# A state-space mixer in steps of two positions, inside a two-block transformer kernel

## The chip, the cores and the metric

The kernel runs on one core of one Trainium2 chip, in one launch. The metric is the device time in microseconds; the median of three runs is given. Engines are named as in the profile: PE is TensorE (matmuls; PEld its weight loads), DVE is VectorE, ACT is ScalarE, POOL is GpSimd, SP is SyncE, whose queue issues the weight loads from HBM.

## The reference, cut to what matters

Two transformer blocks run over one sequence of 256 positions of width 2048, in float32. The second block has three branches: a gated MLP over positions, the state-space mixer (S5) and a stick-breaking attention. In the mixer, 64 groups of 16 channels each drive 64 complex diagonal states:

```python
dt = jnp.exp(log_dt)[:, None]
mag = jnp.exp(lam_re * dt)
ab_re = mag * jnp.cos(lam_im * dt)          # the step a, complex
ab_im = mag * jnp.sin(lam_im * dt)
...
bu_re = jnp.einsum('blgh,gph->blgp', u, bb_re)
bu_im = jnp.einsum('blgh,gph->blgp', u, bb_im)
# associative scan over positions: s[t] = a * s[t-1] + bu[t]
_, _, s_re, s_im = lax.associative_scan(combine, (a_re, a_im, bu_re, bu_im), axis=1)
y = (jnp.einsum('blgp,ghp->blgh', s_re, c_re) - jnp.einsum('blgp,ghp->blgh', s_im, c_im))
y = y.reshape(bsz, seq, S5_WIDTH) + d * xin
g = jax.nn.gelu(y)
out = g * jax.nn.sigmoid(g @ w_glu + b_glu)
```

## The kernel before, in words

Every wide product is made from float32 weights split in two parts: ACT writes the high half `wh` in a reduced matmul format (fp32r; L213), DVE the rest, `wl` (L214), and PE adds three products, weights' high by activations' high and low, and low by high. Weights come in pieces of 512 KB that SP's queue loads.

In the first part of the second block (`block2`) the projection's columns are worked off in the order `ORDER2`: U and W for the gated MLP, C for the mixer's input, V and Q for the attention, G for gates. Each of these steps yields after a few matmuls with the PE time that they were planned at. Between the steps the loop in `block2` hands out other work by that planned time: one step of the mixer (`states`, the generator `rest`) for every 3.9 us (`RS`), and one step of the attention or gating chains for every 0.52 us (`RC`). What then stands where on each engine's queue is set by a planner that puts the instructions in order by a simulated timeline. Each engine works its queue in order.

The mixer (`s5`) keeps two groups side by side on the 128 partitions, so there are 32 blocks of 128 states (real and imaginary part each), in 8 groups of four (`ct`). A setup computes steps, powers of the rotation (`ek`) and input matrices `bb`. Then, for each group `ct`, `prepare` spreads the matrices B and C into block form by ACT and PE transposes, splits them in high and low, and POOL builds the table `tab` of the rotation's powers for 128 positions by doubling. For each block `i`:

- `drive(i)`: PE multiplies the block's input (`xin`, 32 channels as high and low halves on 64 partitions, 256 positions) by B: 4 matmuls of 256 columns into a PSUM bank `bu`.
- `scan(i)`: DVE turns the drive back by the table (two products over 128x512, an add and a subtract over 128x256). What is left is a real recurrence with factor |a|, which DVE's scan instruction runs (L2002). The table reaches over 128 positions, so the 256 are scanned in two halves, with three small instructions that carry the state over (L1998 to L2000): four scans. POOL turns the result forward again with two products over 128x512 (L2004, L2005).
- `result(i)`: an add and a subtract over 128x256 finish the turn; for two blocks of four (`CO` = 2) DVE does them, for the others POOL. ACT writes the high half `sh`, POOL the low half `sl` (L2017). PE multiplies both by C into the group's bank: 4 matmuls of 256 columns. After the fourth block DVE adds the bank to `y` (L2029, four instructions).

PSUM banks for all of this come from `pmx`, four that go round, shared with the attention and gating chains.

Of the kernel before, what the change touches and what calls it, by code (L numbers as in the profile page):

```python
# [18 lines left out]
T = 256  # L19
# [9 lines left out]
def _consts():  # L29
    p = np.arange(128)[:, None]  # L30
    f = np.arange(128)[None, :]
    t = np.arange(T)[None, :]
    c = {}
    c["ident"] = p == f
    c["bd64"] = (p // 64) == (f // 64)
    for d in (128, 64):
        half = d // 2
        inv = np.float32(10000.0) ** (-np.arange(half, dtype=np.float32) * np.float32(2.0 / d))
        ang = np.arange(T, dtype=np.float32)[:, None] * inv.astype(np.float32)[None, :]
        cos = np.cos(ang).astype(np.float32).T  # L40
# [18 lines left out]
    c["tril"] = p >= f  # L59
    c["ntril"] = np.where(p >= f, -1.0e30, 0.0)  # L60
# [10 lines left out]
C3 = ("geq", "strict", "tril", "ntril", "half", "odd")  # L71
# [44 lines left out]
class Ker:  # L116
# [1366 lines left out]
    LO, CO = (0, 2)  # L1483
# [157 lines left out]
    def gmlp(self, y, w_in, vp, chains):  # L1641
# [62 lines left out]
    def sb(self, y, w_in, vp, chains):  # L1704
# [29 lines left out]
        def heads(j, q, k, pre):  # L1734
# [15 lines left out]
            for i, w in enumerate(work):  # L1750
# [6 lines left out]
                nc.vector.tensor_add(dg(zs), dg(zs), b2(c["ntril"]))  # L1757
# [41 lines left out]
    def s5(self, y, w_in, st):  # L1799
# [6 lines left out]
        with ExitStack() as s1:  # L1806
# [91 lines left out]
        def cols(j):  # L1898
# [17 lines left out]
        mats = []  # L1916
        for i in range(2):

            mats.append([p.tile([128, 640], F32R, name=f"C{i}{a}") for a in range(2)])
            for m in mats[i]:  # L1920
                G.memset(m.bitcast(F32), 0.0)

        def prepare(ct):

            tabs[ct] = tab = p.tile([128, 2, 4, H], F32, name="tab", bufs=2)
            Cm = mats[ct % 2]
            B = [[p.tile([128, 2, 128], F32R, name=f"B{x}{a}", bufs=2) for x in "hl"] for a in range(2)]
            blocks[ct] = B, Cm
            for a in range(2):
                rb = p.tile([128, 4, 2, 2, 16], F32, name="rb")  # L1930
                rc = p.tile([128, 2, 64], F32, name="rc")
                for e in range(2):
                    nc.scalar.activation(rb[:, :, :, e], bb[:, a, 4 * ct:4 * ct + 4][:, :, None, :].to_broadcast([128, 4, 2, 16]),
                                         AF.Copy, scale=c["half"][:, e:e + 1])
                    nc.scalar.activation(rc[:, e], cc[:, a, ct], AF.Copy, scale=c["odd"][:, e:e + 1])
                ps = self.pmx()
                for g in range(2):
                    nc.tensor.transpose(ps[:, ts(g, 128)], rb[:, 2 * g:2 * g + 2].rearrange("p k d e h -> p (k d e h)"),
                                        self.ident)
                nc.tensor.transpose(ps[:, 256:384], rc.rearrange("p e n -> p (e n)"), self.ident)  # L1940
                self.split(*(t.rearrange("p g n -> p (g n)") for t in B[a]), ps[:, 0:256])
                ch = Cm[a].rearrange("p (k n) -> p k n", k=4)[:, :, 0:32]
                pc = ps[:, 256:384].rearrange("p (k n) -> p k n", k=4)
                nc.scalar.activation(ch, pc, AF.Copy)
                for g, o in ((0, 64), (1, 256)):
                    k2 = slice(2 * g, 2 * g + 2)
                    V.tensor_sub(Cm[a][:, o:o + 320].rearrange("p (k n) -> p k n", k=2)[:, :, 0:32], pc[:, k2],
                                 ch[:, k2].bitcast(F32))
# [3 lines left out]
            for k in range(7):  # L1952
                n = 1 << k
                er, ei = (ek[:, k, a, 4 * ct:4 * ct + 4][:, :, None].to_broadcast([128, 4, n]) for a in range(2))
# [11 lines left out]
        hv = lambda t: t.rearrange("p a (c t) -> p a c t", c=2)  # L1966
        w2 = lambda nm, bufs: p.tile([128, 2, T], F32, name=nm, bufs=bufs)
        bus, posts, ypss = {}, {}, {}

        def drive(i):  # L1970

            ct, k = divmod(i, 4)
            B, rows, g = blocks[ct][0], slice(64 * (k % 2), 64 * (k % 2) + 64), k // 2
            xi = xins[ct // 2][rows, g, ts(ct % 2, T)]
            bu = bus[i] = self.pmx()
            for a in range(2):
                for x in range(2):
                    self.mm(bu[:, ts(a, T)], B[a][x][rows, g], xi, start=a == x == 0, stop=a == x == 1)

        def tables(i):  # L1980
            ct, k = divmod(i, 4)
            tab = tabs[ct]
            return [tab[:, a, k][:, None, None, :].to_broadcast([128, 2, 2, H]) for a in range(2)]

        def scan(i):
            cb, sb = tables(i)
            bv = bus.pop(i).rearrange("p (a t) -> p a t", a=2)
# [18 lines left out]
            posts[i] = b1, z  # L2006

        def result(i):
# [5 lines left out]
            sh = p.tile([128, 2, T], F32R, name="sh", bufs=self.SB)  # L2014
            sl = p.tile([128, 2, T], F32R, name="sl", bufs=self.SB)
# [4 lines left out]
            yps, Cm = ypss[ct], blocks[ct][1]  # L2020
            for a in range(2):
                for x in (sh, sl):
                    self.mm(yps[:, ts(k // 2, T)], Cm[a][:, ts(k, 128)], x[:, a], start=k % 2 == 0 and a == 0 and x is sh,
                            stop=k % 2 == 1 and a == 1 and x is sl)
            if k == 3:
                for g in range(2):
# [145 lines left out]
```

## Time and profile before

| | before |
|---|---|
| median of 3 runs | 2947.54 us (2946.69 to 2952.38) |
| the profiled execution's own time | 2951.56 us |
| its span, first to last instruction | 2949.4 us |
| PE busy | 2832.4 us (96%) |
| DVE busy | 2105.3 us (71%) |
| ACT busy | 1612.5 us (55%) |
| POOL busy | 455.1 us (15%) |
| mean granted PE clock | 0.990 |

An engine's busy time is the time covered by its instructions. Matmuls are pipelined and their ends are modelled, so a busy PE is not PE at its peak. The shares are means over stages that differ; the mixer's stage lies from about 1330 us to 1762 us of the span.

### The profile page before, as it was taken

Reading aid. Unit: us, or ns where it says so; the run is one execution under the profiler, and the core shown is the slowest. Engines: PE = TensorE matmul, PEld = TensorE weight load, DVE = VectorE, ACT = ScalarE, POOL = GpSimd, SP = SyncE. Lnnn points to the kernel's source line nnn. Section 1 sums busy time; section 2 is a strip of 40 time slices with the busy share of each in tenths; the row PEclk is TensorE's granted clock in tenths of the full one; section 3 lists DMA queues with packets and bytes.
Section 4 is the critical chain, followed back from the end, with each engine's and each line's share of the span. In section 5 each row is a group of like instructions: output and inputs, shape, how many; then the busy total and the mean of one; then the engine's idle time right before and its main releaser. Section 6 shows DMA issues by size and latency. Waiting matters only on the chain. (4 is left out here: it accounts for less than half of the span.)

```text
span 2949.4 us, 45262 instructions
## 1 busy us (share of the span) xinstructions
PE 2832.4 (96%) x17284; PEld 2493.9 (85%) x17284; DVE 2105.3 (71%) x2898; ACT 1612.5 (55%) x2161; POOL 455.1 (15%) x623
## 2 busy tenths in 40 slices
PE   8999999997999999998888789999999999999998
PEld 8998989876887788787677789999988888888887
DVE  7685876647998999898999986555555654456554
ACT  6466466536777777765444445444445553345443
POOL 1111111011000000018898840000000000000000
PEclk9999999998999999999999999999999999999999
DMA  6444443484989999864434336666556666666665
GB/s 196 132 118 120 119 118 104 128 285 150 380 296 350 378 379 357 305 176 142 122 115 122 100 110 196 187 187 186 186 186 197 189 188 194 194 189 186 192 193 171
DMA packets 400512, 576.77 MB, mean 196 GB/s; under 512 B 25032, under 2 KB 252624, under 8 KB 400160
## 3 DMA queue, kind: packets, MB, share of 16 engines
q1 hardware_dynamic: 397632, 567.74, 59.6%
q0 software_dynamic: 2624, 6.06, 0.8%
q8 instruction: 137, 2.24, 0.3%
q14 instruction: 87, 0.71, 0.1%
q10 hardware_dynamic: 32, 0.01, 0.0%
HBM read 571.64 MB, written 2.10 MB: 195 GB/s over the span
## 5 line engine op out<-in xcount | busy, mean ns | idle before, releaser
L214 DVE TENSOR_TENSOR wl<-raw,wh 128x1024 fp32r<-128x1024 f32 (+1 forms) x917 | 1133.7, 1241 | 624.5 <-ACT wh L213 604.6
L213 ACT ACTIVATE wh<-raw 128x1024 fp32r<-128x1024 f32 (+1 forms) x917 | 965.2, 1055 | 900.8 <-PE acc L223 686.6
L223 PE MATMUL acc<-hx,wh 128*128 128x256 f32 (+3 forms) x5280 | 1149.8, 306 | 0.5 <-ACT hx L347 0.2
L223 PE MATMUL acc<-hx,wl 128*128 128x256 f32 x3152 | 890.1, 284 | 13.1 <-DVE wl L214 13.0
L223 PEld LDWEIGHTS acc<-hx,wh 128*128 128x128 f32 (+2 forms) x5280 | 849.7, 189 | 55.4 <-issue 8.0
L223 PEld LDWEIGHTS acc<-hx,wl 128*128 128x128 f32 x3152 | 592.8, 188 | 24.1 <-DVE wl L214 15.3
L214 DVE TENSOR_TENSOR wl<-rx,wh 128x1024 fp32r<-128x1024 f32 x159 | 191.3, 1223 | 26.9 <-ACT wh L213 13.6
L223 PE MATMUL acc<-wl,xgh 128*128 128x512 f32 x512 | 201.2, 394 | 2.5 <-DVE wl L214 2.5
L223 PE MATMUL acc<-wh,xgh 128*128 128x512 f32 x512 | 200.1, 391 | 2.9 <-ACT wh L213 2.9
L223 PE MATMUL acc<-wh,xgl 128*128 128x512 f32 x512 | 200.4, 392 | 0.0
L223 PE MATMUL acc<-wh,al 128*128 128x512 f32 x512 | 199.2, 389 | 0.0
L223 PE MATMUL acc<-wh,ah 128*128 128x512 f32 x512 | 199.2, 389 | 0.0
L213 ACT ACTIVATE wh<-rx 128x1024 fp32r<-128x1024 f32 x159 | 167.6, 1061 | 55.9 <-PE acc L223 36.4
L223 PE MATMUL acc<-wl,ah 128*128 128x512 f32 x512 | 179.2, 389 | 0.0
L223 PE MATMUL mx<-wh,act 128*128 128x512 f32 x512 | 140.3, 394 | 1.5 <-DVE act L220 0.8
L223 PE MATMUL acc<-wh,hx 128*128 128x512 f32 x384 | 122.6, 402 | 0.0
L223 PEld LDWEIGHTS acc<-wl,xgh 128*128 128x128 f32 x512 | 96.2, 188 | 25.4 <-DVE wl L214 5.3
L223 PEld LDWEIGHTS mx<-wh,act 128*128 128x128 f32 x512 | 96.6, 189 | 23.2 <-DVE act L220 1.2
L223 PEld LDWEIGHTS acc<-wh,xgh 128*128 128x128 f32 x512 | 96.2, 188 | 23.1 <-ACT wh L213 4.1
L223 PEld LDWEIGHTS acc<-wl,ah 128*128 128x128 f32 x512 | 96.1, 188 | 20.0
L223 PEld LDWEIGHTS acc<-wh,xgl 128*128 128x128 f32 x512 | 96.2, 188 | 19.9
L223 PEld LDWEIGHTS acc<-wh,ah 128*128 128x128 f32 x512 | 96.1, 188 | 19.9
(589 smaller groups left out, 4149.2 us busy)
## 6 DMA issues: line engine op xcount, KB each, us to landing
raw<-in_w_in_dram SPq DMA_DIRECT2D x304, 512.0 KB, 3.7
raw<-in_w_mlp_in_dram SPq DMA_DIRECT2D x128, 512.0 KB, 3.8
raw<-in_w_mlp_out_dram SPq DMA_DIRECT2D x128, 512.0 KB, 3.8
raw<-in_w_e_gate_dram SPq DMA_DIRECT2D x80, 512.0 KB, 6.0
raw<-in_w_e_down_dram SPq DMA_DIRECT2D x77, 512.0 KB, 6.0
raw<-in_w_e_up_dram SPq DMA_DIRECT2D x75, 512.0 KB, 5.7
raw<-in_w_out_dram SPq DMA_DIRECT2D x57, 512.0 KB, 3.8
rx<-in_w_e_up_dram SPq DMA_DIRECT2D x53, 512.0 KB, 6.4
```

What stands on the lines that cost most here:

```text
L213: self.lasth = nc.scalar.activation(h[:, :n], raw[:, :n], AF.Copy).ins
L214: self.lastl = nc.vector.tensor_sub(l[:, :n], raw[:, :n], h[:, :n].bitcast(F32)).ins
L223: return self.nc.tensor.matmul(out, lhsT, rhs, start=start, stop=stop)
```

## The change

The mixer steps over pairs of positions. States are kept at even positions only (0, 2, ..., 254): 128 of them, so one table covers them all and the second half with its joins goes away. The recurrence becomes s[2t] = a² s[2t-2] + (a B) u[2t-1] + B u[2t], so the drive takes the even inputs and the odd ones before them, with matrices B and a B, on all 128 partitions. The output at even positions is C s[2t], at odd ones (C a) s[2t] + (C B) u[2t+1], from matrices C a one step later and a direct product D = C B of the odd input. `xin` gets a new layout: odd inputs, shifted by one pair, on partitions 0 to 63, even ones on 64 to 127. `prepare` makes more matrices and asks for five PSUM banks where it asked for two. The result's add and subtract are done by DVE for all blocks (`CO` = 4). Two constants of the attention are dropped, one of them replaced by a scalar times the mask `geq` at L1757, the scratch for descriptors of POOL's DMAs is made smaller, and the loads of `br` and `bi` are cut in two.

```diff
-    LO, CO = (0, 2)
+    LO, CO = (0, 4)
...
-                nc.vector.tensor_add(dg(zs), dg(zs), b2(c["ntril"]))
+                nc.vector.scalar_tensor_tensor(dg(zs), b2(c["geq"]), -1.0e30, dg(zs), op0=OP.mult, op1=OP.add)
...
+            ab = p.tile([128, 2, 32], F32, name="ab")
+            V.tensor_mul(ab, ek[:, 0], sc[:, 0:1].to_broadcast([128, 2, 32]))
+            m2 = p.tile([128, 32], F32, name="m2")
+            V.tensor_mul(m2, sc[:, 0], sc[:, 0])
...
-            nc.gpsimd.dma_start(br, A["s5_b_re_2"][0].rearrange(pat, a=2))
-            nc.gpsimd.dma_start(bi, A["s5_b_im_2"][0].rearrange(pat, a=2))
+            for s in (0, 16):
+                for t_, n in ((br, "re"), (bi, "im")):
+                    nc.gpsimd.dma_start(t_[:, s:s + 16], A[f"s5_b_{n}_2"][0, 2 * s:2 * s + 32].rearrange(pat, a=2))
...
+            ka = lambda k: ab[:, k][:, :, None].to_broadcast([128, 32, 16])
+            V.tensor_mul(bb[:, 0, 0], b0, ka(0))
+            V.tensor_mul(t3, b1, ka(1))
+            V.tensor_sub(bb[:, 0, 0], bb[:, 0, 0], t3)
+            V.tensor_mul(bb[:, 1, 0], b1, ka(0))
+            V.tensor_mul(t3, b0, ka(1))
+            V.tensor_add(bb[:, 1, 0], bb[:, 1, 0], t3)
...
+            xins[j] = xin = p.tile([128, 2, 4, H + 2], F32R, name="xin", bufs=self.XB)
+            G.memset(xin[0:64, :, :, 0:1].bitcast(F32), 0.0)
             for k in range(4):
-                o = 64 * (k % 2)
-                h, l, f = slice(o, o + 32), slice(o + 32, o + 64), slice(32 * k, 32 * k + 32)
-                nc.scalar.activation(xin[h, k // 2], xn[f], AF.Copy)
-                V.tensor_sub(xin[l, k // 2], xn[f], xin[h, k // 2].bitcast(F32))
+                xn = yj[32 * k:32 * k + 32].rearrange("p a (c t) -> p a c t", t=2)
+                for o, c0, t in ((0, 1, 1), (64, 0, 0)):
+                    h, l = (xin[o + d:o + d + 32, :, k, c0:c0 + H] for d in (0, 32))
+                    nc.scalar.activation(h, xn[:, :, :, t], AF.Copy)
+                    V.tensor_sub(l, xn[:, :, :, t], h.bitcast(F32))
...
+                for k in range(4):
+                    nc.tensor.transpose(ps[:, ts(k, 128)], rb[:, k].rearrange("p t d e h -> p (t d e h)"), self.ident)
+                self.split(*(t.rearrange("p g n -> p (g n)") for t in B[a]), ps)
+                ps = self.pmx()
+                nc.tensor.transpose(ps[:, 0:128], rc.rearrange("p e n -> p (e n)"), self.ident)
+                nc.scalar.activation(cf[:, a, :, 0], ps[:, 0:128].rearrange("p (k n) -> p k n", k=4), AF.Copy)
+            yield
+
+            ar, ai = (ab[:, x, 4 * ct:4 * ct + 4][:, :, None].to_broadcast([128, 4, 32]) for x in range(2))
+            tc_ = p.tile([128, 4, 32], F32, name="tc")
+            for o, x, y0, op in ((0, ar, ai, G.tensor_add), (1, ai, ar, G.tensor_sub)):
+                G.tensor_mul(tc_, cf[:, 0, :, 0], x)
+                G.tensor_mul(cf[:, o, :, 1], cf[:, 1, :, 0], y0)
+                op(cf[:, o, :, 1], cf[:, o, :, 1], tc_)
+            self.split(*(t.rearrange("p a k t n -> p (a k t n)") for t in C), cf.rearrange("p a k t n -> p (a k t n)"))
+            ps = self.pmx()
+            for k in range(4):
+                for a in range(2):
+                    self.mm(ps[0:64, ts(k, 32)], rbs[a][:, k, 1].rearrange("p d e h -> p (d e h)"), cf[:, a, k, 0],
+                            start=a == 0, stop=a == 1)
+            self.split(D[0][:, :, 32:64], D[1][:, :, 32:64], ps[0:64, 0:128].rearrange("p (k n) -> p k n", k=4))
...
-            xi = xins[ct // 2][rows, g, ts(ct % 2, T)]
+            xi = xins[ct // 2][:, ct % 2, k, 0:H]
             bu = bus[i] = self.pmx()
             for a in range(2):
                 for x in range(2):
-                    self.mm(bu[:, ts(a, T)], B[a][x][rows, g], xi, start=a == x == 0, stop=a == x == 1)
+                    self.mm(bu[:, ts(a, H)], B[a][x][:, k], xi, start=a == x == 0, stop=a == x == 1)
...
-            a1, a2 = w2("a1", 2), w2("a2", 1)
-            V.tensor_mul(hv(a1), hv(bv), cb)
-            V.tensor_mul(hv(a2), hv(bv), sb)
+            a1, a2 = w2("a1", 2), w2("a2", 2)
+            V.tensor_mul(a1, bv, cb)
+            V.tensor_mul(a2, bv, sb)
             V.tensor_add(a1[:, 0], a1[:, 0], a2[:, 1])
             V.tensor_sub(a1[:, 1], a1[:, 1], a2[:, 0])
             z = w2("z", 2)
-            mg = sc[:, 0, i:i + 1].to_broadcast([128, H])
-            for c0 in (0, H):
-                if c0:
-                    x0, z0 = a1[:, :, H:H + 1], z[:, :, H - 1:H]
-                    stt(x0, z0, eh[:, 0, i:i + 1], x0, op0=OP.mult, op1=OP.add)
-                    stt(x0[:, 0], z0[:, 1], eh[:, 2, i:i + 1], x0[:, 0], op0=OP.mult, op1=OP.add)
-                    stt(x0[:, 1], z0[:, 0], eh[:, 1, i:i + 1], x0[:, 1], op0=OP.mult, op1=OP.add)
-                for a in range(2):
-                    V.tensor_tensor_scan(z[:, a, c0:c0 + H], mg, a1[:, a, c0:c0 + H], 0.0, op0=OP.mult, op1=OP.add)
+            mg = m2[:, i:i + 1].to_broadcast([128, H])
+            for a in range(2):
+                V.tensor_tensor_scan(z[:, a], mg, a1[:, a], 0.0, op0=OP.mult, op1=OP.add)
             b1 = w2("b1", 2)
-            G.tensor_mul(hv(b1), hv(z), cb)
-            G.tensor_mul(hv(z), hv(z), sb)
+            G.tensor_mul(b1, z, cb)
+            G.tensor_mul(z, z, sb)
...
-            sh = p.tile([128, 2, T], F32R, name="sh", bufs=self.SB)
-            sl = p.tile([128, 2, T], F32R, name="sl", bufs=self.SB)
+            sh = p.tile([128, 2, H], F32R, name="sh", bufs=self.SB)
+            sl = p.tile([128, 2, H], F32R, name="sl", bufs=self.SB)
...
+            o = yps[0:64, ts(k, H)]
+
+            xi = xins[ct // 2][0:64, ct % 2, k, 1:1 + H]
+            self.mm(o, D[0][:, k], xi, start=True, stop=False)
+            self.mm(o, D[1][:, k], xi, start=False, stop=False)
             for a in range(2):
-                for x in (sh, sl):
-                    self.mm(yps[:, ts(k // 2, T)], Cm[a][:, ts(k, 128)], x[:, a], start=k % 2 == 0 and a == 0 and x is sh,
-                            stop=k % 2 == 1 and a == 1 and x is sl)
+                ch, cl = (x[:, a, k].rearrange("p t n -> p (t n)") for x in C)
+                self.mm(o, ch, sh[:, a], start=False, stop=False)
+                self.mm(o, cl, sh[:, a], start=False, stop=False)
+                self.mm(o, ch, sl[:, a], start=False, stop=a == 1)
             if k == 3:
-                for g in range(2):
-                    for o in (64 * g, 64 - 64 * g):
-                        yo = y[64 * g:64 * g + 64, 8 + ct]
-                        V.tensor_add(yo, yo, yps[o:o + 64, ts(g, T)])
+                for g in range(4):
+                    yo = y[32 * g:32 * g + 32, 8 + ct].rearrange("p (c t) -> p c t", t=2)
+                    for t in range(2):
+                        V.tensor_add(yo[:, :, t], yo[:, :, t], yps[32 * t:32 * t + 32, ts(g, H)])
...
-    nc = bacc.Bacc("TRN2", target_bir_lowering=False, num_devices=1)
+    nc = bacc.Bacc("TRN2", target_bir_lowering=False, num_devices=1, dynamic_dma_scratch_size=4096)
```

## Rows read from the trace of the kernel before

**Rows 1.** busy us (instructions) of PE, PEld, DVE, ACT, POOL; clock, DMA share, GB/s

```profile
0.00:1330.00 1330.00, 1290.05 (x7709) 1115.11 (x7710) 1043.80 (x1553) 865.46 (x1151) 101.45 (x135) 0.99 0.68 227
1330.00:1762.00 432.00, 364.20 (x2372) 323.43 (x2371) 398.41 (x653) 194.18 (x327) 352.98 (x487) 0.96 0.39 118
1762.00:2949.40 1187.40, 1178.19 (x7209) 1055.36 (x7207) 663.11 (x694) 552.91 (x684) 0.62 (x1) 1.00 0.61 188
```

**Rows 2.** two 40 us stretches, same columns

```profile
1560.00:1600.00 40.00, 34.09 (x186) 27.41 (x184) 39.86 (x63) 17.59 (x30) 39.33 (x57) 1.00 0.38 113
...
1800.00:1840.00 40.00, 40.00 (x342) 40.00 (x341) 25.33 (x27) 16.90 (x18) 0.00 (x0) 1.00 0.60 186
```

**Rows 3.** PE's waits, 1330 to 1762: total us, times, longest

```profile
PE mx L223 <- POOL sl L2017: 20.2, 15, 4.6
PE acc L223 <- DVE wl L214: 18.3, 12, 7.4
PE mx L223 <- ACT sh L2016: 8.9, 7, 2.2
```

**Rows 4.** tile `a` (DVE), then `b` (DVE, ACT, POOL), 1330 to 1762

```profile
1330.00:1762.00 432.00, 185.61 (x352) 0.96 0.39 118
...
1330.00:1762.00 432.00, 18.00 (x32) 20.12 (x32) 132.39 (x96) 0.96 0.39 118
```

**Rows 5.** DVE's groups by line, 1330 to 1770: busy, mean ns, idle before

```profile
L2002 DVE TENSOR_TENSOR_SCAN z<-sc,a 128x128 f32<-128x128 f32 x128 | 74.3, 617 | 0.1
L1992 DVE TENSOR_TENSOR a<-a,a 128x256 f32<-128x256 f32 x32 | 23.5, 735 | 0.0
...
L2029 DVE TENSOR_TENSOR y<-y,mx 64x256 f32<-64x256 f32 x32 | 13.3, 416 | 0.6
```

**Rows 6.** DVE's groups by line and form, whole span

```profile
L2084 DVE TENSOR_TENSOR r<-acc,lo 128x256 f32<-128x256 f32 x64 | 27.0, 421 | 19.4 <-ACT lo L2083 19.4
...
L1098 DVE TENSOR_TENSOR P<-mx,sc 128x128 f32<-128x128 f32 x8 | 2.3, 286 | 4.2 <-PE mx L223 4.2
```

**Rows 7.** single lines: count, ns min/median/max, first and last start

```profile
L1989 DVE TENSOR_TENSOR a<-mx,tab x32: 658/678/692, 1357.9 to 1730.1; 128x512 f32<-128x512 f32 x32
...
L1991 DVE TENSOR_TENSOR a<-a,a x32: 394/418/1499, 1361.7 to 1733.4; 128x256 f32<-128x256 f32 x32
...
L2002 DVE TENSOR_TENSOR_SCAN z<-sc,a x128: 386/413/1505, 1362.7 to 1744.9; 128x128 f32<-128x128 f32 x128
```

**Rows 8.** tile `tab` (DVE, POOL), 1330 to 1762; POOL groups by form

```profile
1330.00:1762.00 432.00, 41.33 (x64) 268.61 (x416) 0.96 0.39 118
...
L2004 POOL TENSOR_TENSOR b<-z,tab 128x512 f32<-128x512 f32 x32 | 52.1, 1629 | 40.1 <-DVE z L2002 33.6 <-DVE vr L317 3.4 <-DVE vr L314 3.0
...
L2017 POOL TENSOR_TENSOR sl<-b,sh 128x512 fp32r<-128x512 f32 x32 | 47.0, 1469 | 21.4 <-ACT sh L2016 21.4
...
L1959 POOL TENSOR_TENSOR tab<-tab,ttmp 128x256 f32<-128x256 f32 x8 | 7.6, 951 | 0.0
```

**Rows 9.** PE timeline (start, us, instructions), three places

```profile
1800.10 0.28 PE L223 MATMUL acc<-y2h,wl 128*128 128x256 f32 x1
...
1803.99 0.28 PE L223 MATMUL acc<-y2h,wl 128*128 128x256 f32 x1
...
105.83 1.95 PE L223 MATMUL mx<-Z,nl 128*128 128x128 f32 x16
107.53 0.36 PE L223 MATMUL acc<-hx,wl 128*128 128x256 f32 x1
...
1597.84 0.38 PE L223 MATMUL mx<-sh,C 128*128 128x256 f32 x1
1598.15 0.38 PE L223 MATMUL mx<-xin,Bl 64*128 64x256 f32 x1
```

**Rows 10.** a setup load (KB, us to landing); POOL timeline

```profile
bi<-in_s_b_im_dram POOLq DMA_DIRECT2D x1, 256.0 KB, 7.8
...
1331.54 0.95 POOL L1891 DMA_DIRECT2D cc<-in_s_c_re_dram  x1 [41.41 <-DVE eh L1874]
```

More of the change, by code (lines that the diff above doesn't have):

```diff
@@ L58, in _consts @@
     c["strict"] = p < f
-    c["tril"] = p >= f
-    c["ntril"] = np.where(p >= f, -1.0e30, 0.0)
     c["half"] = (p // 64) == np.arange(2)[None, :]
@@ L70 @@
 C2 = ("iota", "before")
-C3 = ("geq", "strict", "tril", "ntril", "half", "odd")
+C3 = ("geq", "strict", "half", "odd")
 def const_arrays():
@@ L1915, in s5 @@
         tabs, blocks = {}, {}
[L1916 to L1921, printed above, removed]
+        own = [[p.tile([64, 4, 64], F32R, name=f"D{i}{x}") for x in "hl"] for i in range(2)]
+        for o in own:
+            for d in o:
+                G.memset(d.bitcast(F32), 0.0)
         def prepare(ct):
             tabs[ct] = tab = p.tile([128, 2, 4, H], F32, name="tab", bufs=2)
-            Cm = mats[ct % 2]
-            B = [[p.tile([128, 2, 128], F32R, name=f"B{x}{a}", bufs=2) for x in "hl"] for a in range(2)]
-            blocks[ct] = B, Cm
+            B = [[p.tile([128, 4, 128], F32R, name=f"B{x}{a}", bufs=2) for x in "hl"] for a in range(2)]
+            C = [p.tile([128, 2, 4, 2, 32], F32R, name=f"C{x}", bufs=2) for x in "hl"]
+            D = own[ct % 2]
+            blocks[ct] = B, C, D
+            cf = p.tile([128, 2, 4, 2, 32], F32, name="cf")
+            rbs = []
@@ L1929, in prepare @@
             for a in range(2):
-                rb = p.tile([128, 4, 2, 2, 16], F32, name="rb")
+                rb = p.tile([128, 4, 2, 2, 2, 16], F32, name=f"rb{a}")
+                rbs.append(rb)
                 rc = p.tile([128, 2, 64], F32, name="rc")
                 for e in range(2):
-                    nc.scalar.activation(rb[:, :, :, e], bb[:, a, 4 * ct:4 * ct + 4][:, :, None, :].to_broadcast([128, 4, 2, 16]),
-                                         AF.Copy, scale=c["half"][:, e:e + 1])
+                    for t in range(2):
+                        nc.scalar.activation(rb[:, :, t, :, e], bb[:, a, t, 4 * ct:4 * ct + 4][:, :, None, :]
+                                             .to_broadcast([128, 4, 2, 16]), AF.Copy, scale=c["half"][:, e:e + 1])
@@ L1953, in prepare @@
                 n = 1 << k
-                er, ei = (ek[:, k, a, 4 * ct:4 * ct + 4][:, :, None].to_broadcast([128, 4, n]) for a in range(2))
+                er, ei = (ek[:, k + 1, a, 4 * ct:4 * ct + 4][:, :, None].to_broadcast([128, 4, n]) for a in range(2))
                 c0, s0 = tab[:, 0, :, 0:n], tab[:, 1, :, 0:n]
@@ L1964, in prepare @@
                     yield
-        hv = lambda t: t.rearrange("p a (c t) -> p a c t", c=2)
-        w2 = lambda nm, bufs: p.tile([128, 2, T], F32, name=nm, bufs=bufs)
+        w2 = lambda nm, bufs: p.tile([128, 2, H], F32, name=nm, bufs=bufs)
         bus, posts, ypss = {}, {}, {}
@@ L1972, in drive @@
             ct, k = divmod(i, 4)
-            B, rows, g = blocks[ct][0], slice(64 * (k % 2), 64 * (k % 2) + 64), k // 2
-            xi = xins[ct // 2][rows, g, ts(ct % 2, T)]
+            B = blocks[ct][0]
+            xi = xins[ct // 2][:, ct % 2, k, 0:H]
             bu = bus[i] = self.pmx()
@@ L1982, in tables @@
             tab = tabs[ct]
-            return [tab[:, a, k][:, None, None, :].to_broadcast([128, 2, 2, H]) for a in range(2)]
+            return [tab[:, a, k][:, None, :].to_broadcast([128, 2, H]) for a in range(2)]
         def scan(i):
             cb, sb = tables(i)
-            bv = bus.pop(i).rearrange("p (a t) -> p a t", a=2)
-            a1, a2 = w2("a1", 2), w2("a2", 1)
-            V.tensor_mul(hv(a1), hv(bv), cb)
-            V.tensor_mul(hv(a2), hv(bv), sb)
+            bv = bus.pop(i)[:, 0:2 * H].rearrange("p (a t) -> p a t", a=2)
+            a1, a2 = w2("a1", 2), w2("a2", 2)
+            V.tensor_mul(a1, bv, cb)
+            V.tensor_mul(a2, bv, sb)
             V.tensor_add(a1[:, 0], a1[:, 0], a2[:, 1])
@@ L2019, in result @@
                 ypss[ct] = self.pmx()
-            yps, Cm = ypss[ct], blocks[ct][1]
+            yps, (_, C, D) = ypss[ct], blocks[ct]
+            o = yps[0:64, ts(k, H)]
+            xi = xins[ct // 2][0:64, ct % 2, k, 1:1 + H]
+            self.mm(o, D[0][:, k], xi, start=True, stop=False)
+            self.mm(o, D[1][:, k], xi, start=False, stop=False)
             for a in range(2):
-                for x in (sh, sl):
-                    self.mm(yps[:, ts(k // 2, T)], Cm[a][:, ts(k, 128)], x[:, a], start=k % 2 == 0 and a == 0 and x is sh,
-                            stop=k % 2 == 1 and a == 1 and x is sl)
+                ch, cl = (x[:, a, k].rearrange("p t n -> p (t n)") for x in C)
+                self.mm(o, ch, sh[:, a], start=False, stop=False)
+                self.mm(o, cl, sh[:, a], start=False, stop=False)
+                self.mm(o, ch, sl[:, a], start=False, stop=a == 1)
             if k == 3:
-                for g in range(2):
-                    for o in (64 * g, 64 - 64 * g):
-                        yo = y[64 * g:64 * g + 64, 8 + ct]
-                        V.tensor_add(yo, yo, yps[o:o + 64, ts(g, T)])
+                for g in range(4):
+                    yo = y[32 * g:32 * g + 32, 8 + ct].rearrange("p (c t) -> p c t", t=2)
+                    for t in range(2):
+                        V.tensor_add(yo[:, :, t], yo[:, :, t], yps[32 * t:32 * t + 32, ts(g, H)])
         def states():
```

29 lines of the change are left out of this document (7 added, 22 removed).

## The prediction

> **What bounds the kernel now.** I cut the span in three by the stretches view. Before 1330 us and after 1762 us TensorE (PE) is busy nearly all the time; between them, while the state-space mixer runs, it is busy 364.2 of 432 us, at a mean granted clock of 0.96 where the rest has 0.99 and 1.00 [rows 1]. Two losses can be read there: 67.8 us in which PE does nothing, and 0.04 x 432 = 17 us of clock. Outside this stretch only a short setup changes, so 85 us, plus what PE itself must do less, is all that can be won.
>
> Who holds PE up? In the stretch VectorE (DVE) is busy 398.4 of 432 us and GpSimd (POOL) 353.0 [rows 1]. In the 40 us from 1560 on DVE works 39.9, POOL 39.3, and PE has 34.1; 240 us later, with DVE at 25.3 and POOL idle, PE is full [rows 2]. The waits of PE say the same by name: for the low half `sl` that POOL makes 20.2 us, for the weights' low half `wl` of L214, which stands in DVE's queue behind the mixer, 18.3, for the high half `sh` 8.9 [rows 3]. So here DVE's queue sets the pace and POOL is a close second; PE is third.
>
> **DVE: what goes.** Everything that writes or reads the tile `a` (two table products, add, subtract, four scans, three joins, each for 32 blocks) fills 185.6 us; the half of the result's add and subtract that DVE does (tile `b`) 18.0 [rows 4]; the 32 additions into `y` (L2029) 13.3 [rows 5]. Together 216.9 us.
>
> **DVE: what comes.** Five groups of 64 instructions. Products: 128x256 out of PSUM, 421 ns in a row of that form [rows 6], 26.9 us. Scans: 64 of the same 128x128 form instead of 128, at the median 413 ns [rows 7] 26.4 us, at the mean 617 [rows 5] 39.5 us. Add and subtract: 128x128; a clean one takes 286 ns [rows 6], 18.3 us. The result's add and subtract, now for all blocks on DVE: the same, 18.3. Additions into `y`: 32x128 with a step of two; no such row, so from 286 ns to the 416 ns of the 64x256 form [rows 5], 18.3 to 26.6 us. The clean sum is 108 us.
>
> The upper end comes from DVE's waits. An operation with both inputs in SBUF, like the subtract at L1992, means 735 ns [rows 5], while its twin L1991 has a median of 418 and a maximum of 1499; the product at L1989, which reads PSUM, never leaves 658 to 692 [rows 7]. So some 0.317 us of waiting hangs on an average one. If the shorter ones wait as long, add, subtract, and the result's pair cost 603 ns each, 38.6 us a group, and the whole is 26.9 + 39.5 + 38.6 + 38.6 + 26.6 = 170 us. DVE saves between 47 and 109 us; I take 80, the middle, since the POOL instructions they wait for get shorter too. The splits of inputs and matrices handle about the same elements (twice as many inputs at half the width, wider B, fewer C): nothing, give or take 10 us. DVE comes to 318 us (279 to 361).
>
> The Trainium skill ("SBUF — State Buffer", Who interferes with whom) says that a DVE instruction with two SBUF inputs contends with a GpSimd instruction that reads SBUF, and that the loser blocks for the whole instruction. The maxima above agree: 1499 ns is a clean subtract plus most of a POOL product. The rule speaks against moving the other 16 pairs of the result from POOL to DVE: by it they cost toward 603 ns, not 286, which is 32 x 0.317 = 10 us of DVE; it also frees POOL of the same work.
>
> **POOL.** It gives up its result pairs, and its two products and the low half shrink to 128x256. Tables and products together fill 268.6 us [rows 8], of which the 64 products (1.629 us each at L2004) are about 104. At the 128x256 table row, 951 ns [rows 8], products come to 61, and the low half goes from 32 x 1.469 = 47 to about 30. New are 48 operations for the odd C matrices at 128x128; half that row's size, so at most 951 ns each, 46 us. With the result pairs (about 34 us: the 353.0 of the stretch less 268.6, less 47 and a few) gone, POOL does 43 + 17 + 34 - 46 = 48 us less, about 305. It does not become the bound.
>
> **PE.** Before: 8 matmuls of 256 columns per block, 256 in all; at the 3.89 / 33 = 0.118 us from start to start [rows 9] that is 30 us. After: 12 of 128 columns, 384 in all. The trace has no 128-column matmul in this reduced format. Lower bound: half of 0.118, 23 us. Upper: full-precision ones of 128 columns, 16 in 1.70 us, 0.106 each [rows 9], 41 us. I take the upper price for the 128 that carry full 128-column weights and 0.08, the middle, for the 256 with 64 columns: 13.6 + 20.5 = 34. Preparing takes 32 transposes more and 64 small products: 96 at up to 0.106, 10 us, or half that. So PE gains 14 us (from -2 to +21).
>
> **Banks, order, start.** Preparation asks for five PSUM banks per group instead of two, with the same four to go round: some waits on banks stay. The setup adds six 128x512 products and two small ones on DVE, about 4 us near 1320, where PE has a queue of wide matmuls; taken at 1. The program still hands out mixer steps by PE time, so their places do not move. In the attention chain L1757 becomes another form of the same size: nothing.
>
> **The sum.** PE's need without losses is 432 - 68 - 17 = 347; with its additions 361. DVE at 318 and POOL at 305 both lie below that, so PE becomes the longest, but not at once free: each block is still a chain DVE, POOL, DVE, ACT, POOL, PE, in queues with other work. Of the 68 us of waits I keep 25 (the share tied to `sl`, `sh` and banks, shorter), of the 17 of clock 6, and 1 for the start. 347 + 14 + 25 + 6 + 1 = 393, 39 us less than 432. The profiled execution lasted 2951.6 us around a span of 2949.4, and the median of the runs is 2947.5, 4 lower; against that median, 2947.5 - 39 = 2908 us. The likeliest case runs from 25 to 65 us won (2882 to 2923).
>
> **Rivals.**
> *All losses go.* Waits and clock nearly vanish and PE's additions are at their lower end: 65 to 85 us won, about 2872. For it: after 1762 PE is full with DVE at 63% of the time [rows 2]. Against: the chain remains. Chance 0.10.
> *The chain still holds.* DVE gets lighter, but what PE waits for is the length of the chain, and the low halves are as late as before: of the 68 us 45 stay, of the 17 of clock 12. 347 + 14 + 45 + 12 + 1 = 419, 13 us won, 2935 (6 to 25 us won). For it: `sl` and `sh` are 29 us of PE's waits [rows 3], and POOL is nearly as loaded as DVE [rows 1]. Against: every link of the chain is halved in size. Chance 0.14.
> *Slower: narrow matmuls.* PE pays per matmul, not per column. Where shape changes, starts lie 0.31 us apart (1597.84 to 1598.15) [rows 9]. At 0.22 each the 384 cost 84 us, 54 more than the 30 of before, with preparation 64: 347 + 64 + 31 + 1 = 443, 11 us longer, 2959. It decides from where the additions reach 85 - 32 = 53 us, that is (30 + 53 - 10) / 384 = 0.19 us for one. Against: most of the 384 follow another of the same shape. Chance 0.13, of it 0.06 within the measurable.
> *A late load.* The smaller descriptor scratch makes POOL's loads wait for one another: POOL idles 41.4 us between the setup's work and the mixer's first load, and the load of `bi` lands after 7.8 us [rows 10]. Ten loads one behind the other would end 78 us after the first, 37 past that gap, and DVE would stand in order behind their first use: that eats the gain, 2945. Chance 0.03.
>
> **Numbers.** The likeliest case has 0.60. A change under 0.2% (5.9 us) is not told apart from none here. Faster: 0.60 + 0.10 + 0.14 = 0.84. Same: 0.06 from the narrow matmuls and 0.02 of the late load, 0.08. Slower: 0.08 (0.07 and 0.01). The range leaves out about 0.2: from 2872, the far end of the best case, to 2938, which takes in most of the chain rival.
>
> **What would show it.** In the mixer's stretch: shorter by about 39 us; DVE near 318 us, POOL near 305; `wl` gone from the top of PE's waits, `sl` below 15 us; starts of the 128-column matmuls no more than 0.11 us apart. The prediction is wrong if those starts lie 0.2 apart, if DVE's two-input operations still mean over 600 ns, or if PE's idle time in the stretch stays above 50 us.

## The result, and the profile after

The changed kernel takes 2911.24 us (median of 4 runs, 2905.99 to 2914.62) where the kernel before takes 2949.02 (4 runs): a ratio of 0.9869, 95% interval 0.985 to 0.9889. A later set gave 2908.98 us and 0.9863. The prediction was 2908. Some runs of the old mixer are 10 to 17 us shorter than the rest; the one of these that was profiled is shorter after 1760 us, where nothing was edited (last section). They bear on the medians of the first, fifth and sixth experiment.

The stretches view of the kernel after; the second row ends where the first product of the branches starts on DVE, a mark that both kernels have:

```profile
1330.00:1762.00 432.00, 410.29 (x2987) 377.05 (x2986) 331.80 (x603) 240.53 (x438) 269.11 (x507) 0.96 0.45 136
1330.00:1758.30 428.30, 406.59 (x2956) 373.35 (x2955) 329.93 (x602) 238.59 (x437) 269.11 (x507) 0.96 0.45 135
```

The same view of the kernel before, to the same mark:

```profile
1330.00:1796.20 466.20, 397.63 (x2652) 356.66 (x2651) 424.35 (x684) 221.54 (x372) 352.98 (x487) 0.96 0.41 123
```

The mark comes 37.9 us earlier; the span is 37.9 us shorter. The whole gain lies between 1330 us and the mark. Split each row into idle time (length less PE's busy time), clock (busy time times what the clock lacks of 1) and the rest, which is what PE needs at full clock. Before: 68.6 + 15.9 + 381.7. After: 21.7 + 16.3 + 390.3. Idle time fell by 46.9, the clock gave nothing back, and PE needs 8.6 more (the clock's two digits leave about 2 us between the last two). Against [rows 1], DVE went from 398.4 to 331.8 and POOL from 353.0 to 269.1.

PE's waits after, 1330 to 1762, answering to [rows 3]:

```profile
PE mx L221 <- POOL sl L2034: 10.5, 7, 2.2
...
PE acc L221 <- DVE wl L212: 2.2, 2, 1.4
PE acc L221 <- ACT wh L211: 2.0, 1, 2.0
PE mx L221 <- ACT sh L2033: 1.7, 1, 1.7
...
PE mx L1956 <- ACT rc L1950: 1.3, 1, 1.3
```

`wl` has all but gone, `sl` has halved. The groups by line after (busy us, mean ns, idle before), DVE then POOL, answering to [rows 5, 8]:

```profile
L212 DVE TENSOR_TENSOR wl<-raw,wh 128x1024 fp32r<-128x1024 f32 x110 | 142.3, 1296 | 53.4 <-ACT wh L211 49.9 <-PE mx L221 3.1
L2019 DVE TENSOR_TENSOR_SCAN z<-m,a 128x128 f32<-128x128 f32 x64 | 29.4, 501 | 0.0
L2052 DVE TENSOR_TENSOR y<-y,mx 32x128 f32<-32x128 f32 x64 | 17.9, 280 | 1.4 <-PE mx L221 0.6
L2029 DVE TENSOR_TENSOR b<-b,z 128x128 f32<-128x128 f32 x32 | 14.2, 445 | 19.9 <-POOL z L2022 19.8
L2030 DVE TENSOR_TENSOR b<-b,z 128x128 f32<-128x128 f32 x32 | 13.2, 411 | 0.0
L2012 DVE TENSOR_TENSOR a<-mx,tab 128x256 f32<-128x256 f32 x32 | 13.1, 416 | 7.2 <-PE mx L221 3.6 <-POOL tab L1983 3.5
...
L2014 DVE TENSOR_TENSOR a<-a,a 128x128 f32<-128x128 f32 x32 | 11.0, 345 | 0.3
...
L2022 POOL TENSOR_TENSOR z<-z,tab 128x256 f32<-128x256 f32 x32 | 31.7, 993 | 0.9
L2021 POOL TENSOR_TENSOR b<-z,tab 128x256 f32<-128x256 f32 x32 | 29.0, 907 | 37.0 <-DVE z L2019 37.0
L2034 POOL TENSOR_TENSOR sl<-b,sh 128x256 fp32r<-128x256 f32 x32 | 27.6, 864 | 28.3 <-ACT sh L2033 28.1
L1965 POOL TENSOR_TENSOR cf<-cf,tc 128x128 f32<-128x128 f32 x16 | 10.6, 665 | 0.2
L1964 POOL TENSOR_TENSOR cf<-cf,ab 128x128 f32<-128x128 f32 x16 | 8.6, 555 | 0.0
L1963 POOL TENSOR_TENSOR tc<-cf,ab 128x128 f32<-128x128 f32 x16 | 8.2, 510 | 8.6 <-ACT cf L1957 8.6
```

DVE now waits 49.9 us for ACT's `wh` in its largest group. PE's timeline after (start, length), the drives of one block and the last of a block's results:

```profile
1461.50 0.27 PE L221 MATMUL mx<-xin,Bl 128*128 128x128 f32 x1
1461.61 0.28 PE L221 MATMUL mx<-xin,Bh 128*128 128x128 f32 x1
1461.72 0.27 PE L221 MATMUL mx<-xin,Bl 128*128 128x128 f32 x1
...
1636.79 0.22 PE L221 MATMUL mx<-sl,Ch 128*64 128x128 f32 x1
1636.85 0.22 PE L221 MATMUL mx<-sh,Ch 128*64 128x128 f32 x1
1636.91 0.22 PE L221 MATMUL mx<-sh,Cl 128*64 128x128 f32 x1
```

A drive costs 0.11 us from start to start, a result matmul 0.06.

### The profile page after: what moved, and what is told of

Its sections match the earlier page's. It is cut to its first block, busy times and chain, and to the rows that moved or that the text cites. A ratio compares the mean times of both kernels' runs of the same rounds, so it can differ in the third digit from the quotient of the medians.

```text
span 2911.5 us, 45852 instructions
## 1 busy us (share of the span) xinstructions
PE 2842.6 (98%) x17572; PEld 2511.9 (86%) x17572; DVE 2010.1 (69%) x2808; ACT 1628.6 (56%) x2225; POOL 371.9 (13%) x645
## 4 chain that ended last, share of the span: by engine, by line
PE 49%; POOL 6%; DVE 1%; issue 1%; DMA 0%; ACT 0%; ACTq 0%; POOLq 0%; DVEq 0%
PE acc L221 47%; PE mx L221 2%; POOL ttmp L1982 1%; POOL ttmp L1985 1%; POOL tab L1983 1%; POOL tab L1986 1%; POOL tab L1984 1%; POOL z L2022 1%; POOL b L2021 1%; POOL tab L1981 0%; POOL sl L2034 0%; POOL cf L1965 0%; DMA cc<-in_s_c_im_dram 0%; PE mx L344 0%; DVE xr L1419 0%
```

## The experiments

The program orders its queues anew for every kernel, so an edit also moves other work a little. What is compared is therefore the median, and the split of the row from 1330 us to the mark:

| kernel | edit | DVE busy | POOL busy | PE idle | mark at | median us |
|---|---|---|---|---|---|---|
| before | | 424.4 | 353.0 | 68.6 | 1796.2 | 2947.5, 2947.6, 2949.2 |
| e1 | before, no joins | 420.3 | 350.7 | 60.0 | 1794.1 | 2936.03 |
| e2 | before, all result pairs on DVE | 418.5 | 315.2 | 59.7 | 1791.5 | 2945.37 |
| e5 | before, one POOL product less | 397.5 | 297.6 | 47.3 | 1772.8 | 2927.41 |
| e6 | before, both left out | 389.1 | 299.6 | 44.1 | 1771.0 | 2918.19 |
| after | | 329.9 | 269.1 | 21.7 | 1758.3 | 2911.24 |
| e4 | after, again | 327.1 | 268.5 | 23.6 | 1753.6 | 2908.98 |
| e3 | after, half the pairs on POOL | 323.5 | 287.6 | 21.5 | 1755.5 | 2910.06 |
| e7 | after, a POOL product twice | 336.0 | 300.4 | 28.9 | 1762.0 | 2916.35 |
| e8 | after, two DVE products twice | 341.8 | 271.8 | 21.8 | 1753.0 | 2908.09 |
| e9 | after, drives twice | 329.0 | 266.5 | 23.5 | 1764.7 | 2919.55 |
| e10 | after, small doublings once | 336.8 | 242.2 | 19.5 | 1746.8 | 2899.70 |
| e11 | e10, output matrices loaded early | 335.0 | 236.3 | 18.9 | 1745.2 | 2899.14 |
| e12 | e11, low halves on DVE | 335.3 | 207.1 | 19.2 | 1747.0 | 2902.11 |

The three medians of before belong to e1 to e4, e5 to e8 and e9 to e12. Each expectation says what its theories are.

**e1: VectorE alone relieved.** The carry over position 128 is left out of the computation.

```diff
-                if c0:
-                    x0, z0 = a1[:, :, H:H + 1], z[:, :, H - 1:H]
-                    stt(x0, z0, eh[:, 0, i:i + 1], x0, op0=OP.mult, op1=OP.add)
-                    stt(x0[:, 0], z0[:, 1], eh[:, 2, i:i + 1], x0[:, 0], op0=OP.mult, op1=OP.add)
-                    stt(x0[:, 1], z0[:, 0], eh[:, 1, i:i + 1], x0[:, 1], op0=OP.mult, op1=OP.add)
```

> The kernel before without the three small join instructions between the two scan halves (the carry of the state over position 128 is left out). Theory A, DVE's queue set the pace of the mixer before: DVE loses 96 instructions, 36.7 us by the rows of before, and 15 to 35 us of it come back, about 2925 us. Rival B, POOL set it as much as DVE: under 8 us come back, 2940 or more.

Measured: ratio 0.9972 (0.9955 to 0.9989). Even that is not the mixer's: six of the ten runs lie at 2932.9 to 2936.1 and four at 2947.4 to 2951.9, and in the profiled one, of the six, the mark is only 2.1 us early; the rest comes after it. So 96 VectorE instructions, 36.7 us of its busy time before, were worth about 2 us, as rival B said. PE's idle time fell by more, from 68.6 to 60.0 us, but its clock was 0.95 instead of 0.96, which took back some 4 us. The stretch to the mark, then two groups of e1:

```profile
1330.00:1794.10 464.10, 404.15 (x2648) 359.37 (x2647) 420.32 (x587) 221.51 (x371) 350.70 (x487) 0.95 0.40 123
```

```profile
L214 DVE TENSOR_TENSOR wl<-raw,wh 128x1024 fp32r<-128x1024 f32 x96 | 143.9, 1502 | 18.5 <-ACT wh L213 16.3 <-PE acc L223 1.5 <-DVE xin L1909 0.2
...
L1992 DVE TENSOR_TENSOR a<-a,a 128x256 f32<-128x256 f32 x32 | 29.8, 933 | 0.0
```

The same view of the kernel before:

```profile
L214 DVE TENSOR_TENSOR wl<-raw,wh 128x1024 fp32r<-128x1024 f32 x96 | 134.9, 1407 | 13.4 <-ACT wh L213 12.8
...
L1998 DVE SCALAR_TENSOR_TENSOR a<-z,eh,a 128x2 f32<-128x2 f32 x32 | 14.8, 464 | 0.2
...
L2000 DVE SCALAR_TENSOR_TENSOR a<-z,eh,a 128x1 f32<-128x1 f32 x32 | 11.4, 357 | 0.0
...
L1999 DVE SCALAR_TENSOR_TENSOR a<-z,eh,a 128x1 f32<-128x1 f32 x32 | 10.5, 329 | 0.1
```

DVE's busy time fell by 4 us, not 36.7: the joins are gone, but `wl` means 1502 ns instead of 1407 and L1992 933 instead of 735 [rows 5]. A busy time that grows back is partly waiting. For whom, `wl` itself shows; kernel before, 1330 to 1760 us, then 1800 to 2100 us where POOL is idle (ns min/median/max):

```profile
L214 DVE TENSOR_TENSOR wl<-raw,wh x95: 1190/1217/2320, 1329.3 to 1757.0; 128x1024 fp32r<-128x1024 f32 x95
...
L214 DVE TENSOR_TENSOR wl<-raw,wh x107: 1218/1226/1228, 1800.0 to 2099.6; 128x1024 fp32r<-128x1024 f32 x107
```

The same instruction has a spread of 10 ns without POOL and up to 1.1 us on top with it, about one clean POOL product (1262 to 1264 ns at the least at L2004 and L2005). The product that reads PSUM never left 658 to 692 [rows 7]. The joins of the kernel before waited too:

```profile
L1998 DVE SCALAR_TENSOR_TENSOR a<-z,eh,a x32: 187/220/1266, 1365.1 to 1742.3; 128x2 f32<-128x2 f32 x32
L1999 DVE SCALAR_TENSOR_TENSOR a<-z,eh,a x32: 185/210/1244, 1366.6 to 1743.9; 128x1 f32<-128x1 f32 x32
L2000 DVE SCALAR_TENSOR_TENSOR a<-z,eh,a x32: 201/210/1351, 1366.7 to 1744.0; 128x1 f32<-128x1 f32 x32
```

By their least times the 96 come to 18.3 us, half of their busy time: e1 took no more work than that from DVE.

**e2 and e3: work moved between the two.** In the kernel before, the other half of the result's add and subtract goes to DVE; in the changed one, half of it goes back to POOL.

```diff
-    LO, CO = (0, 2)
+    LO, CO = (0, 4)
```

```diff
-    LO, CO = (0, 4)
+    LO, CO = (0, 2)
```

> The kernel before with the result's add and subtract on DVE for all blocks (CO = 4), the one part of the change that moves work between the two engines. Theory A (DVE set the pace): DVE gains 32 instructions of 0.42 to 0.66 us, 13 to 21 us, POOL loses 34; slower by 5 to 15 us, about 2959. Rival B (POOL as much): faster by 5 us or more.

> The changed kernel with half of the result's add and subtract back on POOL (CO = 2). Theory A: after the change DVE has slack and POOL holds up the first 240 us of the mixer, so 32 more POOL instructions (24 to 30 us) cost 5 to 15 us, about 2921. Rival C, DVE still sets the pace: 14 us less DVE work, faster by 3 to 10 us, about 2905.

Measured: e2 0.9992 (0.9982 to 1.0002); e3 2910.06 us, 0.9866 (0.985 to 0.9883), the changed kernel's own time. Neither theory's move came. The stretch of e2 to the mark, then two of PE's waits in it (1330 to 1762), answering to [rows 3]:

```profile
1330.00:1791.50 461.50, 401.85 (x2630) 359.60 (x2629) 418.49 (x710) 220.02 (x370) 315.15 (x454) 0.95 0.39 123
```

```profile
PE acc L223 <- DVE wl L214: 24.0, 12, 7.1
PE mx L223 <- POOL sl L2017: 13.1, 10, 2.4
```

POOL is 37.8 us lighter, and the mark comes only 4.7 us earlier. PE waits less for POOL's `sl` (13.1 us instead of 20.2) and more for `wl`, which stands in DVE's queue (24.0 instead of 18.3). So the added instructions on DVE took back most of what POOL gave.

> The changed kernel itself, as the measure for the other runs beside it: 2911 us, ratio 0.987.

e4, the changed kernel unedited, gave 2908.98 us (0.9847 to 0.988): two sets differ by 2.3 us, so less than that is not read below.

**e5 and e6: GpSimd relieved, and both.** The sine product is left out of the rotation back; e6 leaves out the joins too.

```diff
             G.tensor_mul(hv(b1), hv(z), cb)
-            G.tensor_mul(hv(z), hv(z), sb)
```

> The kernel before, without GpSimd's second product of each block (z times the sine table, 32 instructions, 50 us of GpSimd's time); VectorE's instructions are all there. The way back from the rotation is left out by that much, so the output is another. Theory A (VectorE's queue alone sets the pace): within 4 us of the kernel before, VectorE's busy time in the stretch as before (398 us). Theory B (VectorE and GpSimd hold each other up, so that VectorE's busy time is partly waiting for GpSimd's instruction): the mean scan falls from 617 ns below 540, VectorE's busy time by 20 us or more, and the run is 12 to 30 us shorter. Theory C (the length of the chain of one block): every block's chain loses 1.5 us, the run 5 to 12 us.

> The kernel before, without that product and without the three instructions that join the two halves of a scan: 50 us less for GpSimd and 37 us less for VectorE, both left out of the computation. Theory A: as without the joins alone, at most 12 us shorter. Theory B: 25 to 45 us shorter, more than the two edits give singly. Theory C: 8 to 16 us shorter.

Measured: e5 0.9928 (0.9902 to 0.9954), e6 0.9897 (0.9854 to 0.9941). Two of e6's four runs and one of e5's six are of the shorter kind; the others have medians near 2926.3 and 2927.9. The stretch and two groups of e5, then the stretch of e6:

```profile
1330.00:1772.80 442.80, 395.47 (x2638) 355.37 (x2637) 397.45 (x677) 220.75 (x372) 297.61 (x455) 0.96 0.41 129
```

```profile
L2002 DVE TENSOR_TENSOR_SCAN z<-sc,a 128x128 f32<-128x128 f32 x128 | 65.2, 551 | 0.3
...
L1992 DVE TENSOR_TENSOR a<-a,a 128x256 f32<-128x256 f32 x32 | 17.4, 542 | 0.0
```

```profile
1330.00:1771.00 441.00, 396.94 (x2649) 355.30 (x2649) 389.08 (x587) 222.73 (x372) 299.61 (x455) 0.97 0.42 130
```

With no mixer instruction taken from DVE, its busy time to the mark fell by 27 us (424.4 to 397.5), L1992 from 735 to 542 ns, PE's idle time by 21, and the mark came 23 us earlier. Theory A falls; theory C had at most 12. Theory B held for e5 but for the size of one sign (scans at 551 ns, not below 540), and not for e6: the joins add about 2 us to the product's 23, where it wanted more than the sum. So DVE's queue alone did not set the pace of the kernel before: with POOL relieved, DVE's busy time fell too, and the mark moved.

That POOL alone set it is not shown either. In e2 POOL shed 37.8 us and the mark moved 4.7. PE's idle time, which leaves the clock out, fell by 8.6 us in e1, 8.9 in e2, 21.3 in e5 and 24.5 in e6. The joins are 18.3 us by their least times and the 32 products of e5 (at least 1.262 us each) 40 us, so each, taken out alone, gave about half a us of idle time for each us of work. This would fit two engines that take turns, where the work of both adds up. No run adds work with two SBUF inputs to DVE alone, and two profiles of the changed kernel (after and e4) differ by 4.7 us at the mark, so how the pace divides between the two engines stays open.

**e7, e8, e9: what has room after.** Each doubles work in the changed kernel, e9 with sums twice as large.

```diff
             G.tensor_mul(b1, z, cb)
+            G.tensor_mul(b1, z, cb)
```

```diff
             V.tensor_mul(a2, bv, sb)
+            V.tensor_mul(a1, bv, cb)
+            V.tensor_mul(a2, bv, sb)
```

```diff
-            for a in range(2):
+            for a in (0, 1, 0, 1):
                 for x in range(2):
                     self.mm(bu[:, ts(a, H)], B[a][x][:, k], xi, start=a == x == 0, stop=a == x == 1)
```

> The changed kernel, in which GpSimd makes its first product of each block twice (32 more instructions of 0.907 us, 29 us). The prediction's theory A (GpSimd does not become the bound): 0 to 5 us longer than the changed kernel. Theory B (GpSimd and what waits for it set the pace until its last table, at 1613 us): 15 to 30 us longer.

> The changed kernel, in which VectorE makes its two table products of each block twice (64 more instructions of 0.414 us that read PSUM, 26 us). Theory A (VectorE's queue): 12 to 26 us longer than the changed kernel. Theory B (GpSimd sets the pace, and these products, which read PSUM, do not hold it up): 0 to 8 us longer.

> The changed kernel with every drive matmul issued twice into the same bank (128 more matmuls of 128 columns with 128-column weights, 0.11 us from start to start, 14 us; the sums are twice as large). If TensorE is now the longest (the prediction's step): 10 to 16 us longer than the changed kernel. If GpSimd's or VectorE's queue sets the pace still: 0 to 5 us, since TensorE's 21.7 us of idle time take the matmuls in. If narrow matmuls cost more than their starts show: over 20 us.

Measured, against the changed kernel's 2909 to 2911: e7 +5 to +7 us, e8 -1 to -3, e9 +8 to +11. The stretch of e8, then of e9:

```profile
1330.00:1753.00 423.00, 401.19 (x2920) 367.37 (x2919) 341.76 (x656) 235.60 (x435) 271.81 (x507) 0.96 0.43 135
```

```profile
1330.00:1764.70 434.70, 411.16 (x3054) 378.06 (x3053) 329.04 (x593) 237.08 (x436) 266.45 (x507) 0.97 0.43 131
```

64 more products on DVE cost nothing: it has room for instructions that read PSUM (none with two inputs in SBUF were added). 29 us of POOL cost some 6, less than theory B's 15. 14 us of TensorE cost about 10, at the lower end of the first expectation, and its idle time does not take them in (23.5 beside 21.7 and 23.6). So after the change PE is the longest, as forecast, and POOL is what still costs.

**e10, e11, e12: less for GpSimd.** The first three doublings of the tables are made for all blocks at once, ahead of the mixer (e10); the load of the output matrices moves ahead of the setup's products (e11); the low halves go to DVE (e12).

```diff
+        pre = p.tile([128, 2, 32, 8], F32, name="pre")
+        ptm = p.tile([128, 4, 64], F32, name="ttmp").rearrange("p k (a n) -> p (k a) n", n=8)
+        nc.gpsimd.memset(pre[:, 0, :, 0:1], 1.0)
+        nc.gpsimd.memset(pre[:, 1, :, 0:1], 0.0)
+        for k in range(3):
+            n = 1 << k
+            er, ei = (ek[:, k + 1, a][:, :, None].to_broadcast([128, 32, n]) for a in range(2))
...
-            G.memset(tab[:, 0, :, 0:1], 1.0)
-            G.memset(tab[:, 1, :, 0:1], 0.0)
+            nc.scalar.activation(tab[:, :, :, 0:8], pre[:, :, 4 * ct:4 * ct + 4], AF.Copy)
...
-            for k in range(7):
+            for k in range(3, 7):
```

```diff
+            cc = p.tile([128, 2, 8, 64], F32, name="cc")
+            nc.gpsimd.dma_start(cc[:, 0], A["s5_c_re_2"][0].rearrange(pat, a=8))
+            nc.gpsimd.dma_start(cc[:, 1], A["s5_c_im_2"][0].rearrange(pat, a=8))
             br, bi, t3 = (q.tile([128, 32, 16], F32, name=nm) for nm in ("br", "bi", "t3"))
```

```diff
-    LO, CO = (0, 4)
+    LO, CO = (4, 4)
```

> The changed kernel, in which the first three doublings of the tables (n = 1, 2, 4) are made once for all 32 blocks ahead of the mixer, 18 wider instructions, instead of in each of eight groups; ScalarE copies them in. GpSimd loses 144 small instructions, 46.8 us by their rows, and gains about 8. If GpSimd still sets the pace until its last table (theory B): by the price of the doubled product (29 us for 7) 8 to 12 us shorter than the changed kernel. If TensorE is the longest by now: 0 to 4 us shorter. If the 18 instructions make the mixer start later: up to 5 us longer.

> The same, and the load of the output matrices is issued ahead of the setup's products instead of behind them (its tile moves into the setup's outer pool). The start of the changed kernel lost TensorE 3.4 us of waiting and about as much clock at 1350 to 1360 us, behind that load. If the load is what is late there: 3 to 7 us shorter than with the tables alone. If the first input, or GpSimd's tables, is late next: 0 to 2 us.

> The same again, with the low half of every state (32 instructions of 128x256) on VectorE instead of GpSimd. VectorE has room (26 us of extra products cost it nothing) and the step from ScalarE to GpSimd goes out of the chain. If the wait for the low half (10.5 us of TensorE's 21.7) is GpSimd's queue: 3 to 8 us shorter than without it. If it is the chain, or VectorE's queue takes GpSimd's place: 0 to 6 us longer.

Measured: e10 0.9829 (0.9815 to 0.9842), e11 0.9824 (0.9811 to 0.9837), e12 0.9836 (0.9823 to 0.985). e10 is 9 to 12 us shorter than the changed kernel, as theory B said; e11 adds nothing that can be told, and e12 is 3 us longer than e11, little more than two sets of one kernel differ by. The stretch of e10:

```profile
1330.00:1746.80 416.80, 397.28 (x2942) 363.93 (x2941) 336.81 (x598) 237.43 (x444) 242.21 (x367) 0.98 0.45 138
```

POOL is 27 us lighter, but PE's idle time fell only from 21.7 to 19.5; the clock went from 0.96 to 0.98, which is 16.3 to 7.9 us. So by this pair of profiles most of the 11.5 us by which the mark moved came back as clock. Against e4's profile of the same changed kernel (mark at 1753.6, idle 23.6) it is 6.8 us, 4.1 of them idle time. The total is firm, its division is not, and why the clock gained was not tried apart. In e11 the load is early, and this slice shows what is late next (1340 to 1350 us):

```profile
1340.00:1350.00 10.00, 7.96 (x39) 6.32 (x38) 7.55 (x17) 9.63 (x27) 7.79 (x20) 1.00 0.30 98
```

ACT is busy 9.63 of 10 us, with copies of the inputs (`xin`) and of the first group's matrices, and PE's longest wait of e11 is for `wh`, which stands in ACT's queue:

```profile
PE mx L221 <- POOL sl L2048: 4.8, 6, 1.3
PE acc L221 <- ACT wh L211: 3.5, 1, 3.5
```

In e12 the low half costs PE 0.9 us instead of 4.8, but `wl` goes from 1.6 to 6.3:

```profile
PE acc L221 <- DVE wl L212: 6.3, 5, 3.2
PE mx L221 <- ACT sh L2047: 3.8, 3, 2.1
...
PE mx L221 <- DVE sl L2048: 0.9, 2, 0.6
```

The wait has changed its name: `wl` stands in VectorE's queue, which takes GpSimd's place. e10 and e11 beat both kernels: by about 50 us the one before, by 10 the changed one.

## Why the prediction was right

**The place and the total.** It put the gain into the mixer's stretch, 39 us; 37.9 came, and the likeliest case was the right one. The idle time that stays was put at 25 us and is 21.7.

**What sets the pace: the step that failed.** "So here DVE's queue sets the pace and POOL is a close second" did not hold. Both were nearly full in [rows 2], but a share of DVE's time was waiting for POOL: 37 us of busy time taken from DVE gave 2 us, where DVE's queue as the bound would have given 15 to 35; 50 from POOL gave 23, both 25. Neither engine set the pace alone (e2), and how it divides between them is open. The forecast did not suffer, because the change relieves both. It had seen the waiting ("some 0.317 us of waiting hangs on an average one") and used it for a price, not for the ranking.

**DVE.** Forecast 318 (279 to 361), measured 331.8 from 1330 to 1762 us. That window now holds work that lay behind it before. To the mark, which holds the same work in both, DVE went from 424.4 to 329.9: it saved 94.5 us, where 80 were forecast (47 to 109). The five new groups sum to 122.8 us (products 26.1, scans 29.4, add and subtract 22.0, the result's pair 27.4, `y` 17.9) between the clean 108 and the upper 170. Means of 343 to 445 ns for the two-input forms are far from the 600 that would have refuted it. The Trainium skill ("SBUF — State Buffer", Who interferes with whom), by which a VectorE instruction with two SBUF inputs blocks against a GpSimd instruction that reads SBUF, agrees with the result's pair at 445 and 411 ns against a clean 286. The prediction's upper price for them, 603 ns, was far too high.

**POOL.** Forecast 305, measured 269.1. The products came as reckoned (60.7 against 61), the low half too (27.6 against 30); the odd C matrices took 27.4 instead of the bound of 46 that was put in for them, and the table instructions got about 13 us shorter in all (tile `tab`, less the products); that they meet fewer VectorE instructions would explain it, but was not tried.

**PE.** Drives at 0.11 us as reckoned, results at 0.06 instead of 0.08. PE's need grew by 8.6 instead of 14, inside -2 to 21.

**The clock: a term mis-sized.** Of the clock's loss 6 us were to remain, and 16.3 did, no less than before. (The 17 us of before counted the whole stretch; over PE's busy time alone, 0.04 x 364, they are 15.) In the changed kernel the granted clock still falls where PE idles; after PE's waits at 1351 to 1354 us (kernel after):

```profile
1350.00:1360.00 10.00, 6.65 (x21) 5.05 (x20) 7.26 (x11) 9.02 (x19) 9.61 (x22) 0.66 0.30 86
```

A slice at 0.66 is part 1.2 and part 2.4 GHz, with PE busy 6.65 of its 10 us: 3.35 us of idle time and 6.65 x 0.34 = 2.3 of clock. The kernel before has such a slice too (1380 to 1390 us: 5.55 busy at 0.66). The start, priced at 1 us for products near 1320, cost nothing there: PE is busy 10.00 of 10 us from 1320 to 1330. The 10 us too little for the clock are made good by 5 too much for PE's need, 3 for its idle time and 1 for the start: the sum was right to 1 us, its terms to 10. That they cancelled is luck.

**Rivals.** The chain of blocks (13 us) and all losses gone (65 to 85) did not come. Narrow matmuls were to decide from 0.19 us each; they cost 0.06 to 0.11. Of the late load one part shows: POOL's four loads of `br` and `bi` start 4 to 5 us apart (1276.33, 1280.60, 1285.62 and 1289.79), where the two of before start 1.75 apart, but PE is full from 1280 to 1330 us and loses nothing there. For `rc`, the copy of the matrices loaded last, PE waits 1.3 us, and loading them earlier (e11) gave nothing that can be told.

## What to carry to other kernels

Where two engines are both nearly full, busy shares don't rank them: compare one instruction's minimum, median and maximum in stretches with and without the other engine, and count what exceeds the clean value as waiting. Take work out altogether (here many small instructions, made once in wide form), since moving it from one to the other gave nothing (e2, e3, e12). When a sum comes out right, check its terms by the same split of a row: here the clock and PE's need were both off and cancelled. And profile one kernel twice before a few us of clock or idle time are read as an effect.

## What had not been expected of the hardware

**Two paces of one instruction stream.** After 1760 us PE is nearly always busy at clock 1.00, with the same matmuls in every kernel built on the old mixer. In the profiled run of e1 there are 2561 of them between 1800 and 2090 us:

```profile
1800.00:2090.00 290.00, 290.00 (x2561) 290.00 (x2561) 168.78 (x165) 130.90 (x148) 0.00 (x0) 1.00 0.62 195
```

In the profiled run of e5, and within one of it in those of before, e2 and e6:

```profile
1800.00:2090.00 290.00, 290.00 (x2464) 290.00 (x2463) 159.28 (x154) 126.17 (x143) 0.00 (x0) 1.00 0.60 187
```

That is 0.113 us from start to start instead of 0.118, some 12 us over the whole stretch. DVE's work and the bytes moved are up as well (165 instructions for 154, 195 GB/s for 187), so it is not a matter of records that are missing. It fits the gap between e1's two sorts of run; only the one profiled shows it directly, and what decides between them stays open.

**Weights, not columns.** A matmul of 128 columns with 128-column weights starts 0.11 us after the last, hardly less than 256 columns do (0.118, [rows 9]); with 64-column weights it is 0.06. Halving the columns alone saved TensorE next to nothing; halving the weights of a 128-column matmul did. That the loading of the weights is what bounds these matmuls is not shown: no run has 256 columns with 64-column weights.
